# A mixer's input projections rewritten as one list of blocks: weight splits one block ahead, the gating half moved forward, the keys' products kept in PSUM

## The chip, the cores and the metric

The kernel runs on one core of a Trainium2 chip (trn2). The metric is device time in microseconds, from start to end of one execution; lower is better. Engines are named as the profile names them: PE is TensorE, DVE is VectorE, ACT is ScalarE, POOL is GpSimd, SP issues the DMAs. SBUF is the memory that the engines work in, PSUM the one that PE writes its products to; DVE and ACT can read and write both.

## The reference, cut to what matters

Two decoder layers over 512 tokens of width 1024. Layer 0 mixes tokens with `mixer_ab`; each layer then cross-attends into 256 memory tokens and applies a mixture of 32 experts.

```python
def mixer_ab(x, w_in, mu, w0, ..., w_out):
    p = x @ w_in                                  # 1024 -> 2816 columns
    ps = p[..., :AB_SHIFT_DIM]                    # r, k, v (512 each), w_lo, a_lo (64 each), g_lo (128)
    pu = p[..., AB_SHIFT_DIM:AB_SHIFT_DIM + SG_DIM]
    pv = p[..., AB_SHIFT_DIM + SG_DIM:]
    ps = ps + (token_shift(ps) - ps) * mu
    ya = rwkv7_mix(ps, ...)
    yb = spatial_gating(pu, pv, ln_g, ln_b, ws, bs)
    return jnp.concatenate([ya, yb], axis=-1) @ w_out

def spatial_gating(pu, pv, ln_g, ln_b, ws, bs):
    u = jax.nn.gelu(pu)
    z = jax.nn.gelu(pv).reshape(B, n_chunk, 128, 4, 128)
    z = layer_norm(z, ln_g, ln_b)                 # over each group of 128 channels
    zs = jnp.einsum('gts,bcsgd->bctgd', tril(ws), z) + bs.T[:, :, None]
    return u * zs.reshape(B, S, SG_DIM)

# in rwkv7_mix, per head of 64:
    kk = k * k_k; kk = kk / max(norm(kk), 1e-12)
    k = k * (1.0 + (a - 1.0) * k_a)
    state_t = state_{t-1} * decay - (state_{t-1} @ kk) (kk * a)^T + v k^T;   y_t = state_t @ r_t
```

## The kernel before

The program is written in Python against a tile layer, whose scheduler turns the order of the code and the dependencies into one queue for each engine. Each engine executes its queue strictly in order; an instruction at the head that waits for a semaphore holds all that stand behind it on that engine.

The change lies in the first 210 us: the first half of `mixer`. Precision comes from splitting: every fp32 operand becomes a high part (a cast on ACT, `wh`, `xh`) and a low part (a subtraction, `wl`, `xl`), and a product takes three matmuls, `xh*wh`, `xl*wh` and `xh*wl` (`mm3`, L212 to L214). A *block* here is one output of 128 columns by 512 tokens (or, in the token-major form, one slab of the contraction for four outputs): 24 matmuls of 512 columns. `wsplit` splits the weights of one block: ACT casts `wh` (L218), POOL subtracts `wl` (L219, since `k.lo_eng` is POOL in this stage). There are two buffers for split weights (`k.nsplit = 2`), so a split can run while the block before it is on PE.

Two generators share the stage and are stepped in turn. `filler` runs the projections: the block of `glo` (g_lo), four of r (`take_r`), four of v, and then `spatial`: the token-major projection `ptm` of the gating's second half (four slabs), GELU into `z`, mean and variance of its 16 groups (`bn_stats` L983, `bn_aggr` L984), an inverse root, the norm of z (L990 to L992), and four blocks of u with `gate`, whose matmuls `pz` (L999) take z. `late(...)` holds back what consumes a block's output until the next block's matmuls are written. `prep` builds the recurrence's operands and the inverse of a triangular matrix for each head and chunk:

- `pkk` (L839) spreads the inverse norms over the channels, four times, once for each group p of 128 channels; DVE multiplies (L841) into `kk`, an SBUF buffer of the ring `tmp` (five buffers), and from it makes `KR` (L842) and `Bn` (L846 with kk, L847 with `vv`); POOL makes `Kh` (L848);
- `pab` (L867) multiplies Bn and KR into `Aab`, 32 matrices of 128x128, copied by ACT (L869);
- the 32x32 diagonal blocks are inverted on DVE by a recurrence of 30 steps of two instructions (`pu` L892, `t8` L894), each waiting for the one before; it ends with a copy and two transposes (L898, L901, L900);
- `pC`, `pT`, `pC2`, `pN2`, `pT2` (L912 to L944) build the larger blocks of the inverse from these on PE, with copies by ACT and DVE between them.

`take_r` takes a block of r: ACT and DVE shift it (L758, L759) into `r`, DVE makes `bt` (L956), POOL scales KR (L957), and PE sums bt over the heads into `pbn` (L961). Those sums of the four blocks collect in one PSUM buffer, copied to `bon` after the last (L963).

PSUM has eight buffers in this stage: four with tag "a" (`prep`) and four with tag "b" (the projections, `pbn` and `pz`). Every `psum(...)` takes the next of its tag and waits until its last reader is done. The raw weights come through SP's queue, a megabyte at a time.

After the stage, `front(0)` begins the second half of the mixer with the transposes `ptv` (L1073). Everything behind that point is untouched: the mixer's second half, the cross-attention, and the experts, whose weights stream from memory while PE multiplies.

Of the kernel before, what the change touches and what calls it, by code (L numbers as in the profile page):

```python
# [714 lines left out]
def mixer(k):  # L715
# [6 lines left out]
    with ExitStack() as st:  # L722
# [18 lines left out]
        with ExitStack() as s1:  # L741
# [12 lines left out]
            def tmp(name):  # L754
                return pool.tile([P, T], F32, name=name, tag="tmp", bufs=5)
# [73 lines left out]
            def prep():  # L829
# [7 lines left out]
                for p in range(4):  # L837
                    ps = k.psum("a", name="pkk")
                    E.matmul(ps, selT[0:8, p * P:(p + 1) * P], rT[0:8, :], start=True, stop=True)  # L839
                    kk, kp = tmp("kk"), yb[:, p]  # L840
# [5 lines left out]
                    V.scalar_tensor_tensor(Bn[:, p], kk, -1.0, Bn[:, p], op0=ALU.mult, op1=ALU.mult)  # L846
                    V.tensor_tensor(Bn[:, p], Bn[:, p], vv[:, p], op=ALU.mult)  # L847
# [121 lines left out]
            def spatial():  # L969
                z = pool.tile([P, NT, 512], F32, name="z")  # L970
                wm = pool.tile([P, 4, P], F32, name="wm")
                nc.sync.dma_start(wm, A["sg_wsT"])
                zg = k.bcast(pool, A["sg_ln_g"], 512, "zg", tag="wa")
                zb = k.bcast(pool, A["sg_ln_b"], 512, "zb", tag="wa2")
                bs = k.bcast(pool, A["sg_b"], 512, "bs")
                yield from proj_tm(k, pool, w_in, 2304, xh, xl, NT, "b",
                                   lambda i, ps: S_.activation(z[:, i, :], ps, AF.Gelu_apprx_tanh))
                zst = pool.tile([P, 16, 6], F32, name="zst")
                zmv = pool.tile([P, 16, 2], F32, name="zmv")
                G_.tensor_tensor(wm, wm, tri[:, None, :].to_broadcast([P, 4, P]), op=ALU.mult)  # L980
                for i in range(NT):
                    for g in range(4):
                        V.bn_stats(zst[:, i * 4 + g], z[:, i, g * P:(g + 1) * P])  # L983
                        V.bn_aggr(zmv[:, i * 4 + g], zst[:, i * 4 + g])  # L984
                zr = k.rsqrt(pool, zmv[:, :, 1], 16, 1e-5, "zr")
                for i in range(NT):
                    for g in range(4):
                        n = i * 4 + g
                        s = z[:, i, g * P:(g + 1) * P]
                        V.tensor_scalar(s, s, zmv[:, n, 0:1], zr[:, n:n + 1], op0=ALU.subtract, op1=ALU.mult)  # L990
                    V.tensor_tensor(z[:, i], z[:, i], zg, op=ALU.mult)
                    V.tensor_tensor(z[:, i], z[:, i], zb, op=ALU.add)  # L992

                def gate(g, ps):
                    u = tmp("u")
                    S_.activation(u, ps, AF.Gelu_apprx_tanh)
                    pz = k.psum("b", name="pz")
                    for i in range(NT):
                        E.matmul(pz[:, i * P:(i + 1) * P], z[:, i, g * P:(g + 1) * P], wm[:, g, :], start=True, stop=True)  # L999
                    V.tensor_tensor(yb[:, g, :].rearrange("p (i t) -> p i t", i=NT), pz.rearrange("p (i t) -> p i t", i=NT),  # L1000
                                    bs[:, None, g * P:(g + 1) * P].to_broadcast([P, NT, P]), op=ALU.add)
                    G_.tensor_tensor(yb[:, g, :], yb[:, g, :], u, op=ALU.mult)

                yield from proj_cm(k, pool, w_in, 1792, 512, xh, xl, T, "b", late(gate))
                flush()

# [1177 lines left out]
```

## Time and profile before

| | |
|---|---|
| median of 3 runs | 1944.18 us (1942.24 to 1944.72) |
| the profiled execution's own time | 1946.41 us |
| its span, first to last instruction | 1944.6 us |
| PE busy | 1785.4 us, 92% of the span |
| DVE, ACT, POOL busy | 932.9, 527.8, 283.8 us |
| mean granted clock of PE | 0.965 of full speed |
| first half of the mixer | 0 to 209 us of the span |

A row of a timeline gives the start in us, the duration in us, the engine, the line of the kernel, the operation, what it writes and reads, and in brackets the idle time of that engine just before it and what ended that idle time. Matmuls are pipelined, so their durations overlap; the distance from start to start is what one costs.

### The profile page before, as it was taken

The numbers are of one execution on the slowest core, as the hardware profiler recorded it, in microseconds if no ns is written. First come the engines' busy times: TensorE is split into PE (matmuls) and PEld (weight loads), VectorE is DVE, ScalarE is ACT, GpSimd is POOL, SyncE is SP. The second block draws the span as 40 slices with busy tenths as digits, with TensorE's granted clock in tenths as the row PEclk, the third lists the DMA queues.
The fourth block names the chain that finished last, engine by engine and source line by source line (L and its number), as shares of the span: only waits on it lengthen the run. The fifth ranks groups of instructions, "written<-read, shape, count | busy, mean of one in ns | idle before, by whom it ended". The sixth has DMA issues, their size and how long they took to land. (4 is left out here: it accounts for less than half of the span.)

```text
span 1944.6 us, 23927 instructions
## 1 busy us (share of the span) xinstructions
PE 1785.4 (92%) x9222; PEld 1095.1 (56%) x9222; DVE 932.9 (48%) x2134; ACT 527.8 (27%) x989; POOL 283.8 (15%) x280
## 2 busy tenths in 40 slices
PE   8898989999889999989888999989979999998895
PEld 5687867878734443433338766768863434443432
DVE  5685366754723332332335666484572323332326
ACT  6333222343221111111122655343221111111110
POOL 3542532400100000000031100130020000000002
PEclk9898989999989999999999999999979999999997
DMA  5221017364889999999985200352779999999992
GB/s 190 65 66 55 23 48 233 115 202 164 346 335 418 420 420 420 419 420 419 418 317 174 76 12 23 109 174 87 290 290 386 421 419 419 419 420 420 421 417 99
DMA packets 126022, 514.69 MB, mean 265 GB/s; under 512 B 15520, under 2 KB 49472, under 8 KB 77264
## 3 DMA queue, kind: packets, MB, share of 16 engines
q1 hardware_dynamic: 115152, 486.60, 63.4%
q0 software_dynamic: 7056, 18.12, 2.8%
q10 hardware_dynamic: 3696, 8.41, 1.1%
q8 instruction: 74, 1.21, 0.3%
q14 instruction: 44, 0.36, 0.1%
HBM read 506.19 MB, written 14.70 MB: 268 GB/s over the span
## 5 line engine op out<-in xcount | busy, mean ns | idle before, releaser
L1787 PE MATMUL pu<-wu,xT 128*64 128x512 f32 x1024 | 237.8, 594 | 19.3 <-DMA wu<-in_moe_w_up_dram 19.3
L1787 PE MATMUL pg<-wg,xT 128*64 128x512 f32 x1024 | 231.6, 599 | 1.6 <-DMA wg<-in_moe_w_gate_dram 1.6
L1813 PE MATMUL py<-wd,hh 128*64 128x512 f32 x1024 | 229.3, 596 | 0.0
L1820 DVE SCALAR_TENSOR_TENSOR wy<-py,tab,wy 128x512 fp32r<-128x512 f32 x64 | 45.5, 747 | 284.1 <-ACT wy L1819 283.8
L1793 DVE TENSOR_TENSOR hh<-hh,pu 128x512 f32<-128x512 f32 x32 | 22.0, 688 | 317.0 <-PE pu L1787 317.0
L1787 PEld LDWEIGHTS pu<-wu,xT 128*64 128x64 f32 x1024 | 75.6, 137 | 174.4 <-issue 133.9
L1827 PE MATMUL pc<-wy,wc 128*128 128x512 f32 x480 | 139.9, 422 | 27.3 <-DVE h L1837 27.3
L1776 ACT ACTIVATE xT<-px,ch 128x128 f32<-128x128 f32 x128 | 48.2, 457 | 421.2 <-PE px L1769 383.5
L1787 PEld LDWEIGHTS pg<-wg,xT 128*64 128x64 f32 x1024 | 76.9, 138 | 149.0 <-issue 131.0
L1837 DVE TENSOR_TENSOR h<-h,pc 128x512 f32<-128x512 f32 x240 | 151.1, 681 | 8.6 <-PE pc L1827 8.6
L1813 PEld LDWEIGHTS py<-wd,hh 128*64 128x64 f32 x1024 | 71.2, 137 | 134.5 <-issue 129.7
L1827 PEld LDWEIGHTS pc<-wy,wc 128*128 128x128 f32 x480 | 81.6, 189 | 86.0 <-DVE h L1837 50.1
L1751 POOL DMA_INDIRECT xg<-rows,idx x32 | 33.5, 1046 | 528.9 <-PE px L1769 508.7
L1757 ACT ACTIVATE xg<-xg 128x1024 f32<-128x1024 f32 x32 | 39.7, 1240 | 246.5 <-DMA xg<-rows,idx 223.8
L218 ACT CAST wh<-wt 128x1024 fp32r<-128x1024 f32 x50 | 51.8, 1050 | 92.2 <-PE ptm L214 56.6
L219 DVE TENSOR_TENSOR wl<-wt,wh 128x1024 fp32r<-128x1024 f32 x37 | 48.1, 1306 | 58.3 <-ACT wh L218 57.9
L212 PE MATMUL ptm<-wh,oh 128*128 128x512 f32 x192 | 75.6, 394 | 0.0
L213 PE MATMUL ptm<-wl,oh 128*128 128x512 f32 x192 | 75.0, 391 | 0.0
L214 PE MATMUL ptm<-wh,ol 128*128 128x512 f32 x192 | 75.0, 390 | 0.0
L212 PE MATMUL pcm<-xh,wh 128*128 128x512 f32 x144 | 60.9, 423 | 7.9 <-ACT xh L218 6.9
L214 PE MATMUL pcm<-xh,wl 128*128 128x512 f32 x144 | 59.6, 414 | 0.5 <-DVE wl L219 0.5
L213 PE MATMUL pcm<-xl,wh 128*128 128x512 f32 x144 | 59.6, 414 | 0.2 <-DVE xl L219 0.2
(572 smaller groups left out, 3392.1 us busy)
## 6 DMA issues: line engine op xcount, KB each, us to landing
wg<-in_moe_w_gate_dram SPq DMA_DIRECT2D x128, 1024.0 KB
wu<-in_moe_w_up_dram SPq DMA_DIRECT2D x128, 1024.0 KB
wd<-in_moe_w_down_dram SPq DMA_DIRECT2D x124, 1024.0 KB
wr<-in_ab_w_in_dram SPq DMA_DIRECT2D x8, 1024.0 KB
wr<-in_xa_wkv_dram SPq DMA_DIRECT2D x8, 1024.0 KB
wt<-in_xa_wkv_dram SPq DMA_DIRECT2D x8, 1024.0 KB
wr<-in_xa_wq_dram SPq DMA_DIRECT2D x8, 1024.0 KB
wt<-in_xa_wo_dram SPq DMA_DIRECT2D x8, 1024.0 KB
```

The costliest lines, as they stand in the source:

```text
L212: nc.tensor.matmul(out, lh, rh, start=start, stop=False)
L213: nc.tensor.matmul(out, lh, rl, start=False, stop=False)
L214: nc.tensor.matmul(out, ll, rh, start=False, stop=stop)
L218: k.nc.scalar.copy(hi, src)
L219: (eng or k.low()).tensor_tensor(lo, src, hi.bitcast(F32), op=ALU.subtract)
L1757: self.k.nc.scalar.activation(x[:, :D], x[:, :D], AF.Identity, scale=x[:, D:D + 1], bias=x[:, D + 1:D + 2])
L1776: r = nc.scalar.activation(self.xT[:, kk, :], pk, AF.Identity, scale=gk, bias=bk)
L1787: nc.tensor.matmul(ps[j * M:(j + 1) * M, :], self.xT[:, half * 4 + kk, j * M:(j + 1) * M], w[j][:, kk, :], start=(half == 0 and kk == 0), ...
L1813: nc.tensor.matmul(py[n][j * M:(j + 1) * M, :], self.hT[:, half * 2 + kk, j * M:(j + 1) * M], w[j][:, kk, n * 512:(n + 1) * 512], start=(h ...
L1820: nc.vector.scalar_tensor_tensor(yl, py[n], self.tab()[:, 1:2], yh.bitcast(F32), op0=ALU.mult, op1=ALU.subtract)
L1827: self.k.nc.tensor.matmul(ps, self.C[:, i * P:(i + 1) * P], y, start=start and not last, stop=last)
L1837: k.nc.vector.tensor_add(k.h[:, i, s], k.h[:, i, s], pc)
```

## The change

Five things, all in the first half of `mixer`:

1. `kk` is a PSUM buffer of tag "a" instead of an SBUF buffer of `tmp`, and the products are taken in another order: `kk` is multiplied with `vv` in place, and then with Bn, so that each of the DVE instructions behind L841 has one operand in PSUM.
2. All remaining projections stand in one list of pairs (split, body): r, glo, the gating's second half (`ztm`), v, u. The block of glo moves behind r, and `ztm` moves from behind v to ahead of it.
3. Each block's split is written before the body of the block ahead of it.
4. Statistics and norm of z (`zstats`, `znorm`) are written behind the bodies of v's four blocks (list places 9 to 12), instead of behind the whole projection.
5. The mask of `wm` moves into the first body of `ztm`; statistics are written four at a time ahead of their `bn_aggr`.

```diff
-                    kk, kp = tmp("kk"), yb[:, p]
+                    kk, kp = k.psum("a", name="kk"), yb[:, p]
                     V.scalar_tensor_tensor(kk, Kh[:, p], col("k_k", p), ps, op0=ALU.mult, op1=ALU.mult)
                     V.tensor_tensor(KR[:, p, 0], kk, KR[:, p, 0], op=ALU.mult)
...
-                    V.scalar_tensor_tensor(Bn[:, p], kk, -1.0, Bn[:, p], op0=ALU.mult, op1=ALU.mult)
-                    V.tensor_tensor(Bn[:, p], Bn[:, p], vv[:, p], op=ALU.mult)
+                    V.scalar_tensor_tensor(kk, kk, -1.0, vv[:, p], op0=ALU.mult, op1=ALU.mult)
+                    V.tensor_tensor(Bn[:, p], kk, Bn[:, p], op=ALU.mult)
...
+            def cm(c0, ncols, consume):
+                raw = {}
+                def ops(cb):
+                    if cb % 2 == 0:
...
+                        raw[cb] = k.wchunk(w_in[:, s0:s0 + n].rearrange("(k p) n -> p k n", p=P), (KD, n), name="wr")
+                    return wsplit(k, pool, raw[cb - cb % 2][:, :, cb % 2 * P:cb % 2 * P + P], KD)
+                def body(cb, wh, wl):
+                    ps = k.psum("b", name="pcm")
+                    for kk in range(KD):
+                        mm3(nc, ps, wh[:, kk, :], wl[:, kk, :], xh[:, kk, :], xl[:, kk, :], kk == 0, kk == KD - 1)
+                    consume(cb, ps)
+                return [(partial(ops, cb), partial(body, cb)) for cb in range(ncols // P)]
...
+            def ztm():
...
+                def body(j, wh, wl):
+                    if j == 0:
+                        flush()
+                        sg["ps"] = [k.psum("b", name="ptm") for i in range(NT)]
+                        G_.tensor_tensor(sg["wm"], sg["wm"], tri[:, None, :].to_broadcast([P, 4, P]), op=ALU.mult)
...
+                    if j == 3:
+                        for i, ps in enumerate(sg["ps"]):
+                            S_.activation(sg["z"][:, i, :], ps, AF.Gelu_apprx_tanh)
...
+            def zstats(i):
+                for n in range(i * 4, i * 4 + 4):
+                    V.bn_stats(sg["zst"][:, n], sg["z"][:, i, n % 4 * P:n % 4 * P + P])
+                for n in range(i * 4, i * 4 + 4):
+                    V.bn_aggr(sg["zmv"][:, n], sg["zst"][:, n])
+                if i == 3:
+                    sg["zr"] = k.rsqrt(pool, sg["zmv"][:, :, 1], 16, 1e-5, "zr")
...
             def filler():
-                yield from proj_cm(k, pool, w_in, 1664, P, xh, xl, T, "b", late(take_g))
-                yield from proj_cm(k, pool, w_in, 0, 512, xh, xl, T, "b", late(take_r))
-                yield from proj_cm(k, pool, w_in, 1024, 512, xh, xl, T, "b", late(lambda p, ps: shifted(vv[:, p], ps, 8 + p)))
+                blocks = (cm(0, 512, late(take_r)) + cm(1664, P, late(take_g)) + ztm()
+                          + cm(1024, 512, late(lambda p, ps: shifted(vv[:, p], ps, 8 + p))) + cm(1792, 512, late(gate)))
+                after = {9: (zstats, 0, 1), 10: (zstats, 2, 3), 11: (znorm, 0, 1), 12: (znorm, 2, 3)}
+                w = blocks[0][0]()
+                for j, (_, body) in enumerate(blocks):
+                    ahead = blocks[j + 1][0]() if j + 1 < len(blocks) else None
+                    body(*w)
+                    w = ahead
+                    if j in after:
...
+                    yield
                 flush()
-                yield from spatial()
```

What the scheduler makes of it is shown at three places. Lines of the changed kernel are one higher than before down to the old `spatial` (L841 becomes L842).

PE, from the end of the third projection block after the keys to the next block (glo, r0, r1 are done before this place in the kernel before, r0, r1, r2 in the changed one). Before:

```order
L213 MATMUL pcm<-xl,wh 128x512
L214 MATMUL pcm<-xh,wl 128x512
L867 MATMUL pab<-Bn,KR 128x128 x10
L961 MATMUL pbn<-mixa,bt 128x2 x4
L867 MATMUL pab<-Bn,KR 128x128 x6
L212 MATMUL pcm<-xh,wh 128x512
```

The same place in the changed kernel:

```order
L214 MATMUL pcm<-xl,wh 128x512
L215 MATMUL pcm<-xh,wl 128x512
L868 MATMUL pab<-Bn,KR 128x128 x8
L962 MATMUL pbn<-mixa,bt 128x2 x4
L868 MATMUL pab<-Bn,KR 128x128 x8
L213 MATMUL pcm<-xh,wh 128x512
```

This `pbn` is that of r0 before and that of r1 now; r0's has moved up, behind the second of the three blocks, ahead of the third `pkk`.

DVE, the products of the third and fourth group of channels with the first r blocks. Before:

```order
L842 TENSOR_TENSOR KR<-kk,KR 128x512
L846 SCALAR_TENSOR_TENSOR Bn<-kk,Bn 128x512
L841 SCALAR_TENSOR_TENSOR kk<-Kh,cv,pkk 128x512
L847 TENSOR_TENSOR Bn<-Bn,vv 128x512
L842 TENSOR_TENSOR KR<-kk,KR 128x512
L846 SCALAR_TENSOR_TENSOR Bn<-kk,Bn 128x512
L759 SCALAR_TENSOR_TENSOR r<-pcm,cv,r 128x511
L847 TENSOR_TENSOR Bn<-Bn,vv 128x512
L956 SCALAR_TENSOR_TENSOR bt<-r,cv,yb 128x512
L759 SCALAR_TENSOR_TENSOR r<-pcm,cv,r 128x511
```

In the changed kernel:

```order
L843 TENSOR_TENSOR KR<-kk,KR 128x512
L847 SCALAR_TENSOR_TENSOR kk<-kk,vv 128x512
L842 SCALAR_TENSOR_TENSOR kk<-Kh,cv,pkk 128x512
L848 TENSOR_TENSOR Bn<-kk,Bn 128x512
L843 TENSOR_TENSOR KR<-kk,KR 128x512
L847 SCALAR_TENSOR_TENSOR kk<-kk,vv 128x512
L760 SCALAR_TENSOR_TENSOR r<-pcm,cv,r 128x511
L848 TENSOR_TENSOR Bn<-kk,Bn 128x512
L957 SCALAR_TENSOR_TENSOR bt<-r,cv,yb 128x512
L760 SCALAR_TENSOR_TENSOR r<-pcm,cv,r 128x511
```

The places are the same; in the three instructions behind each L842 `kk` now stands in PSUM.

DVE, the end of the recurrence and what follows it. Before, the recurrence runs out (only the shifts of r and v stand in it) and the statistics of z come behind all four copies of `pN`:

```order
L892 TENSOR_TENSOR pu<-pd_645,t_551 128x30
L894 TENSOR_TENSOR t_551<-t_551,pu 128x30
L898 COPY t_551<-t_551 128x32x32
L901 STREAM_TRANSPOSE b_550<-t_551 128x1024
L900 STREAM_TRANSPOSE b_550<-t_551 128x1024
L915 COPY t_551<-pC 32x512 x2
L925 COPY h<-pT 32x16x32 x2
L938 COPY t_551<-pN_1116 64x512
```

In the changed kernel:

```order
L1038 BN_STATS zst<-z 128x6
L893 TENSOR_TENSOR pu<-pd_656,t_562 128x30
L1038 BN_STATS zst<-z 128x6
L895 TENSOR_TENSOR t_562<-t_562,pu 128x30
L1038 BN_STATS zst<-z 128x6
L899 COPY t_562<-t_562 128x32x32
L902 STREAM_TRANSPOSE b_561<-t_562 128x1024
L901 STREAM_TRANSPOSE b_561<-t_562 128x1024
L760 SCALAR_TENSOR_TENSOR vv<-pcm,cv,vv 128x511
L1040 BN_AGGR zmv<-zst 128x2 x4
L1038 BN_STATS zst<-z 128x6 x4
L1040 BN_AGGR zmv<-zst 128x2 x4
```

Twelve of the sixteen BN_STATS and eight of the BN_AGGR now stand inside the recurrence's last eight steps, the first of them behind the L893 of 184 elements; the rest, the inverse root and the norm stand behind it, between the copies of `pC`, `pT` and `pN`.

## Rows read from the trace of the kernel before

**Rows 1.** Busy time by stretch: PE, PEld, DVE, ACT, POOL, PEclk, DMA share, GB/s

```profile
57.00:90.00 33.00, 25.94 (x112) 18.58 (x112) 25.87 (x36) 10.89 (x17) 19.93 (x13) 0.83 0.13 37
176.00:210.00 34.00, 29.13 (x138) 24.15 (x139) 20.11 (x41) 5.83 (x8) 9.62 (x5) 0.90 0.17 53
600.00:700.00 100.00, 96.00 (x450) 40.17 (x446) 34.63 (x70) 16.47 (x28) 3.78 (x7) 1.00 1.01 420
```

**Rows 2.** Timeline of PE, around the waits ahead of the block of r2

```profile
79.83 0.48 PE L867 MATMUL pab<-Bn,KR 64*128 64x128 f32 x2 [1.66 <-DVE kk L841]
85.62 1.87 PE L961 MATMUL pbn<-mixa,bt 128*128 128x2 f32 x8 [5.31 <-DVE bt L956]
...
89.01 0.79 PE L212 MATMUL pcm<-xh,wh 128*128 128x512 f32 x1
...
96.08 0.95 PE L961 MATMUL pbn<-mixa,bt 128*128 128x2 f32 x8
```

**Rows 3.** Timeline of DVE, the keys' products and the first r

```profile
66.62 0.75 DVE L841 SCALAR_TENSOR_TENSOR kk<-Kh,cv,pkk 128x512 f32<-128x512 f32 x1 [3.82 <-PE pkk L839]
...
83.23 0.68 DVE L847 TENSOR_TENSOR Bn<-Bn,vv 128x512 f32<-128x512 f32 x1
...
85.49 0.74 DVE L759 SCALAR_TENSOR_TENSOR r<-pcm,cv,r 128x511 f32<-128x511 f32 x1
86.27 2.06 DVE L956 SCALAR_TENSOR_TENSOR bt<-r,cv,yb 128x512 f32<-128x512 f32 x1
```

**Rows 4.** Timeline of POOL, one weight split in the same stretch

```profile
84.99 2.80 POOL L219 TENSOR_TENSOR wl<-wr,wh 128x1024 fp32r<-128x1024 f32 x1
```

**Rows 5.** Groups of DVE by form, 57 to 210 us: count, busy us, mean ns

```profile
L846 DVE SCALAR_TENSOR_TENSOR Bn<-kk,Bn 128x512 f32<-128x512 f32 x4 | 6.0, 1506 | 0.0
L842 DVE TENSOR_TENSOR KR<-kk,KR 128x512 f32<-128x512 f32 x4 | 6.0, 1495 | 0.0
...
L983 DVE BATCH_NORM_STATS2 zst<-z 128x6 f32<-128x128 f32 x16 | 4.2, 269 | 2.2 <-ACT z L977 2.2
...
L984 DVE BATCH_NORM_AGGREGATE zmv<-zst 128x2 f32<-128x6 f32 x16 | 2.5, 161 | 0.0
```

**Rows 6.** Timeline of ACT, the table load for glo's sigmoid

```profile
62.64 1.28 ACT L967 ACT_TABLE_LOAD   x1
```

**Rows 7.** Timeline of DVE, the recurrence: first step, r3, 184 elements, end

```profile
107.32 0.20 DVE L892 TENSOR_TENSOR pu<-pd,t 128x30 f32<-128x30 f32 x1
...
109.54 0.74 DVE L759 SCALAR_TENSOR_TENSOR r<-pcm,cv,r 128x511 f32<-128x511 f32 x1
...
128.58 0.36 DVE L892 TENSOR_TENSOR pu<-pd,t 128x184 f32<-128x184 f32 x1
...
136.80 1.19 DVE L900 STREAM_TRANSPOSE b<-t 128x1024 f32<-128x1024 f32 x1
```

**Rows 8.** Timeline of PE, the first pC and the first transpose behind the stage

```profile
138.16 3.63 PE L912 MATMUL pC<-b,Aab 32*32 32x32 f32 x122
...
209.12 0.60 PE L1073 MATMUL ptv<-cst,vv 128*128 128x128 f32 x4
```

**Rows 9.** Timeline of PE, the first pz and the block behind it

```profile
188.73 0.49 PE L999 MATMUL pz<-wm,z 128*128 128x128 f32 x2 [1.36 <-DVE z L992]
192.73 0.80 PE L999 MATMUL pz<-wm,z 128*128 128x128 f32 x2 [3.51 <-DVE z L992]
...
193.75 0.63 PE L213 MATMUL pcm<-xl,wh 128*128 128x512 f32 x1
194.18 0.63 PE L214 MATMUL pcm<-xh,wl 128*128 128x512 f32 x1
...
198.92 0.39 PE L212 MATMUL pcm<-xh,wh 128*128 128x512 f32 x1
199.15 0.40 PE L213 MATMUL pcm<-xl,wh 128*128 128x512 f32 x1
```

**Rows 10.** Groups of POOL by form, 57 to 210 us: the weight splits

```profile
L219 POOL TENSOR_TENSOR wl<-wr,wh 128x1024 fp32r<-128x1024 f32 x11 | 27.7, 2519 | 49.5 <-ACT wh L218 49.5
```

More of the change, by code (lines that the diff above doesn't have):

```diff
@@ L2 @@
 from contextlib import ExitStack, contextmanager
+from functools import partial
 from itertools import islice
@@ L967, in take_g @@
                 S_.activation(glo, glo, AF.Sigmoid)
[L969 to L1005, printed above, removed]
             pend = []
@@ L1018, in late @@
                 return take
-            def filler():
-                yield from proj_cm(k, pool, w_in, 1664, P, xh, xl, T, "b", late(take_g))
-                yield from proj_cm(k, pool, w_in, 0, 512, xh, xl, T, "b", late(take_r))
-                yield from proj_cm(k, pool, w_in, 1024, 512, xh, xl, T, "b", late(lambda p, ps: shifted(vv[:, p], ps, 8 + p)))
+            def cm(c0, ncols, consume):
+                raw = {}
+                def ops(cb):
+                    if cb % 2 == 0:
+                        n = min(2 * P, ncols - cb * P)
+                        s0 = c0 + cb * P
+                        raw[cb] = k.wchunk(w_in[:, s0:s0 + n].rearrange("(k p) n -> p k n", p=P), (KD, n), name="wr")
[6 more added lines that the diff above has]
+                return [(partial(ops, cb), partial(body, cb)) for cb in range(ncols // P)]
@@ new lines, in zstats, with znorm @@
+            def zstats(i):
[5 more added lines that the diff above has]
+                    sg["zr"] = k.rsqrt(pool, sg["zmv"][:, :, 1], 16, 1e-5, "zr")
+            def znorm(i):
+                z = sg["z"]
+                for n in range(i * 4, i * 4 + 4):
+                    t = z[:, i, n % 4 * P:n % 4 * P + P]
+                    V.tensor_scalar(t, t, sg["zmv"][:, n, 0:1], sg["zr"][:, n:n + 1], op0=ALU.subtract, op1=ALU.mult)
+                V.tensor_tensor(z[:, i], z[:, i], sg["zg"], op=ALU.mult)
+                V.tensor_tensor(z[:, i], z[:, i], sg["zb"], op=ALU.add)
@@ new lines, in gate @@
+            def gate(g, ps):
+                u = tmp("u")
+                S_.activation(u, ps, AF.Gelu_apprx_tanh)
+                pz = k.psum("b", name="pz")
+                for i in range(NT):
+                    E.matmul(pz[:, i * P:(i + 1) * P], sg["z"][:, i, g * P:(g + 1) * P], sg["wm"][:, g, :], start=True, stop=True)
+                V.tensor_tensor(yb[:, g, :].rearrange("p (i t) -> p i t", i=NT), pz.rearrange("p (i t) -> p i t", i=NT),
+                                sg["bs"][:, None, g * P:(g + 1) * P].to_broadcast([P, NT, P]), op=ALU.add)
+                G_.tensor_tensor(yb[:, g, :], yb[:, g, :], u, op=ALU.mult)
@@ new lines, in filler @@
+            def filler():
+                blocks = (cm(0, 512, late(take_r)) + cm(1664, P, late(take_g)) + ztm()
[7 more added lines that the diff above has]
+                    if j in after:
+                        f, *ii = after[j]
+                        for i in ii:
+                            f(i)
+                    yield
```

19 lines of the change are left out of this document (added).

## The prediction

> **What bounds the kernel now.** First I read the busy time by stretch [rows 1]: behind the mixer PE is busy 96 us of 100 and the weights stream at a DMA share of 1.01, so nothing there is touched or can be won. In the changed first half, two stretches stand out: 57 to 90 us, with PE busy 25.9 us of 33 at a mean granted clock of 0.83, and 176 to 210 us, 29.1 of 34 at 0.90; DMA is at 0.13 and 0.17, so no load binds. PE's queue is the line to follow: it is in order, and what ends last at its waits sets the time. Its timeline names those waits. At 79.83 PE has waited 1.66 us for a `kk` of DVE, and at 85.62 another 5.31 us for a `bt` of DVE [rows 2]; at 188.73 and 192.73 it has waited 1.36 and 3.51 us for the norm of z [rows 9]. After each pair the clock is at the lower level: matmuls of 512 columns start 0.43 us apart (193.75 to 194.18, 1.2 GHz), against 0.23 us (198.92 to 199.15, 2.4 GHz) [rows 9]. What PE did before the clock fell was to wait. Elsewhere in the stage PE runs through, and DVE's recurrence ends at 136.80 + 1.19 = 137.99 us [rows 7], just as PE reaches `pC` at 138.16 [rows 8]: before the change these two arrive together.
>
> **The products in PSUM.** Why is DVE late at 85.62? Its eight products L842 and L846 take 1.50 us on average [rows 5], while L847, as many elements, takes 0.68 when undisturbed [rows 3]. A split runs on POOL from 84.99 to 87.79 [rows 4]. Within it, L759, which reads PSUM, takes its usual 0.74 us, but L956, with two SBUF tensors, starts at 86.27 and ends at 88.33, after POOL is through [rows 3]. So a DVE instruction with two SBUF tensors stands still while POOL works, and one with a PSUM operand does not. The change gives all twelve products behind L841 a PSUM operand: 8 x (1.50 - 0.68) = 6.6 us go. The chain from the first L841 (66.62) to the fourth Bn (83.23 + 0.68 = 83.91) [rows 3] was 17.3 us; less 6.6, plus the shift and `bt` of r0 that now stand in it (0.7 and 0.7, up to 2.06 if POOL holds the second; I take 2.0 for both), it is 12.7. It starts some 1.5 us earlier, since glo's table load (1.28 us, [rows 6]) and sigmoid no longer stand on ACT ahead of the copy that `pkk` needs. Bn is complete near 77.8, r1's `bt` near 78.5.
>
> PE began to wait at 79.83 - 1.66 = 78.17. It now has one `pbn` more to do ahead of that (0.95 us, [rows 2]), so it comes by at 79 and finds both ready; I leave 0.3 us for a wait. Gone are 1.66 + 5.31 = 7.0 us, and the half clock behind them: 85.62 to 89.01 (`pbn` and six `pab`), half of 3.4 us, is 1.7, and the block from 89.01 to 96.08 took 7.07 us against 24 x 0.23 = 5.5, so 1.6 [rows 2]. Together 10.3 - 0.3 = **10.0 us**: what began at 96.08 begins at 86.1.
>
> An instruction with PSUM operands costs a little more: L841 0.75 against 0.68 for L847 [rows 3], 12 x 0.07 = 0.8 us, off PE's path, since DVE has 0.5 us in hand at each place and the loads of PE are three blocks. The Trainium skill speaks against working in PSUM ("VectorE: DVE Perf Modes", Rules for kernel authors: copy out of PSUM first if many operations follow). By that the products should go back to SBUF, and the 6.6 us would stay; the rows give 0.07 us for each as the price, so here the measurement decides.
>
> **Splits and loads moved ahead.** ACT's cast and POOL's subtraction (2.52 us, [rows 10]) of one block fit well into a block of 5.5 us; with two buffers, a split can't start before the block two places earlier is through, in either order. Cost nothing; if POOL falls a whole block behind, each block would wait up to 2.5 us. The loads keep their number and their places in SP's queue; the first raw tile of r grows to a full megabyte, with the DMA at 0.13 [rows 1]. The mask of `wm` moves on POOL behind a product that is read 30 us later: nothing.
>
> **The gating's second half moved up.** Its four outputs need all four "b" buffers. The third waits for the copy of `bon`, the fourth for the shift of glo, and both stand on DVE in the recurrence. The recurrence's first step follows the last `pab`, so it comes 10.0 us earlier, at 97.3 [rows 7]. glo's shift stands where r3's stood, 109.54 - 107.32 = 2.2 us in, and takes 0.74: 100.3. PE starts `ptm` near 95.5 (86.1, two `pbn`, 16 `pab` of 2 us in all, an estimate, and a block) and reaches the fourth output 18 x 0.23 later, at 99.6: a new wait of **0.7 us** (0 to 2.2).
>
> **Statistics inside the recurrence.** Here a wait is added that has no counterpart before: the first BN_STATS stands on DVE ahead of the last eight steps, and the recurrence's end, `pC` on PE, and everything behind it wait for that. When is z there? `ptm`'s first output is done after 72 + 6 matmuls, at 95.5 + 17.9 + 0.7 = 114.1; the table load (1.28, [rows 6]) and GELU make it 115.8. When does DVE get there? 128.58 - 107.32 = 21.3 us in [rows 7], less some 4.3 for four shifts and a `bt` that left (0.74 each, [rows 7], plus short waits), plus 0.7 for glo: 97.3 + 17.7 = 115.0. It waits 0.8 us. Then 137.99 - 128.58 = 9.4, less 1.0 for the last shift, plus the statistics: 12 x 0.27 + 8 x 0.16 = 4.5 us if each stands in the chain in full [rows 5], 0 if they fill the gaps between dependent steps; nothing in the rows decides, I take 2.3. The end is 115.8 + 8.4 + 2.3 = 126.5.
>
> PE arrives at `pC` at 138.16 - 10.0, less one `pbn` and eight matmuls that are now on the other side (0.9 + 1.8), plus 0.7: near 126.1. So it waits 0.4, and `pC` starts at **126.5**, 11.7 earlier.
>
> **From `pC` to the end of the stage.** That was 209.12 - 138.16 = 71.0 us [rows 8]. Add the eight matmuls, 1.8. In DVE's queue the norm of z now ends some 20 us (an estimate) ahead of `pz`, so 1.36 + 3.51 = 4.9 go, and with them the half clock of the block behind (eleven matmuls at 0.43 for 0.23, 2.2) [rows 9]: 65.7. `ptv` starts at **192.2**, 16.9 us earlier.
>
> **Behind the stage** no instruction changes place, and the first expert weights are issued by progress of the cross-attention, so all of it moves with `ptv`. The sum is made against the profiled execution, 1946.4 us: 1946.4 - 16.9 = 1929.5. That execution stands 2.2 us above the median of the runs, so the median of the changed kernel is **1927 us**. A measurement of this kernel tells about 0.2%, 4 us, from no change.
>
> **Rivals.** *The wait moves to DVE behind the recurrence* (0.18). The statistics cost their full 4.5 us (2.2 more), the third and fourth sets, the inverse root and the norm hold up the copies of `pC` and `pT` in DVE's queue, and PE's clock falls once more after such a wait (2.2, as behind `pz`, [rows 9]). For it: PE has nothing else to do while `pT` waits. Against: PE's own 3.6 us of `pC` [rows 8] cover most of it. 5 us less: 1932. The Trainium skill has a rule that makes it likelier ("SBUF — State Buffer", Who interferes with whom): a one-source DVE instruction in the two-port mode is blocked by POOL too, and POOL copies four pieces into `h` just then. No row here shows that pair; it is one more way to the same 1932.
>
> *PSUM doesn't free the products* (0.05): writing `kk` there costs, or the four "a" buffers make `pkk` and `pab` wait for `kk`. Then 9 of the 10.0 us stay: 1936. Against it: L759 beside the split [rows 3, 4].
>
> *Given back later* (0.05): the weights stream at full share [rows 1]; if their start were bound by something that doesn't move, PE would wait for them: 1944, no change.
>
> *Slower* (0.04): PE's clock stays at 1.2 GHz. Each of the new waits (0.3, 0.7, 0.4) is short, but if one of them drops the clock and it doesn't come back through `ptm` and v, each matmul costs 0.20 us more; 17 us are lost after 85 matmuls, three and a half blocks. Over seven blocks, 168 matmuls, 34 us: 1961. Against: the shortest waits behind which rows show the half clock are 1.36 and 3.51 together, and it came back within eleven matmuls.
>
> **How the numbers follow.** The forecast has 0.68, with its own range of 1924 to 1930 (statistics at 0 or 4.5, `ptm`'s wait at 0 or 2.2, a fall of the clock more or less). With the first rival to 1935, and 2 us on the other side for low-clock runs that vanish besides, the range is 1922 to 1935. Faster by over 0.2%: 0.68 + 0.18 + 0.05 = 0.91; within 0.2%: 0.05; slower: 0.04.
>
> **What would show it.** In the profile of the changed kernel: L843 and L847 (the products with `kk`) at 0.7 us on average; no wait of PE above 0.5 us at `pab` and `pbn`; r3's block at 0.23 us a matmul; a wait of the fourth `ptm` output for glo's shift below 1 us; `pC` at 126 to 128, waiting for DVE; no wait at `pz`; `ptv` near 192. The forecast is wrong if `pC` starts later than 130, if a granted clock below 0.9 shows between 86 and 126, or if `ptv` has moved 17 us and the end has not.

## The result, and the profile after

The changed kernel takes 1932.42 us in the median of four runs (1929.65 to 1937.78), beside 1944.45 us for the kernel before: a ratio of 0.9934 (95% interval 0.9915 to 0.9954), 12.0 us less. Two later series of the same kernel gave 0.9944 and 0.9950 (below); the median of the last, 1935.47, lies 0.5 above the forecast's range. The forecast was 1927, with 1922 to 1935 as its range and 1924 to 1930 as the likeliest case's own: the direction and the mechanism held, the narrower range was missed, and some 5 of the 17 us are missing.

The profiled execution of the changed kernel took 1937.78 us, the longest of its four (span 1935.8). First its waits. Timeline of PE in the changed kernel; columns: start, duration, engine, line, operation, output and inputs, wait:

```profile
81.91 1.16 PE L868 MATMUL pab<-Bn,KR 64*128 64x128 f32 x16
83.00 1.05 PE L962 MATMUL pbn<-mixa,bt 128*128 128x2 f32 x8
83.99 1.16 PE L868 MATMUL pab<-Bn,KR 64*128 64x128 f32 x16
...
90.67 0.95 PE L962 MATMUL pbn<-mixa,bt 128*128 128x2 f32 x8
...
104.95 0.50 PE L213 MATMUL ptm<-wh,xh 128*128 128x512 f32 x1 [0.64 <-DVE glo L760]
...
130.34 3.63 PE L913 MATMUL pC<-b,Aab 32*32 32x32 f32 x122
...
186.40 1.05 PE L1057 MATMUL pz<-wm,z 128*128 128x128 f32 x8
...
192.74 1.05 PE L1057 MATMUL pz<-wm,z 128*128 128x128 f32 x8
...
200.87 0.60 PE L1125 MATMUL ptv<-cst,vv 128*128 128x128 f32 x4
```

The waits of 1.66 and 5.31 us at `pab` and `pbn` [rows 2] and of 1.36 and 3.51 at `pz` [rows 9] are gone. The new wait at the fourth `ptm` output is 0.64 us (0.7 forecast), and `pC` starts without one (0.4 forecast). Yet `pbn` of r2 starts at 90.67, not 86.1, and `pC` at 130.34, not 126.5.

Now the products. Groups of DVE by form in the changed kernel, 57 to 210 us; behind the bar the busy us and the mean ns of one:

```profile
L1038 DVE BATCH_NORM_STATS2 zst<-z 128x6 f32<-128x128 f32 x16 | 4.3, 282 | 0.2 <-ACT z L1032 0.2
...
L847 DVE SCALAR_TENSOR_TENSOR kk<-kk,vv 128x512 f32<-128x512 f32 x4 | 2.7, 686 | 0.0
...
L848 DVE TENSOR_TENSOR Bn<-kk,Bn 128x512 f32<-128x512 f32 x4 | 2.7, 681 | 0.0
L843 DVE TENSOR_TENSOR KR<-kk,KR 128x512 f32<-128x512 f32 x4 | 2.7, 678 | 0.0
```

L843 and L847 take 0.68 and 0.69 us, where the products behind L841 took 1.50 [rows 5]. DVE waits 0.2 us for z in the recurrence, where the forecast had 0.8.

So no wait above 0.3 us is missing from the forecast (0.27 at `pT` is new). What differs is the clock. Timeline of PE in the changed kernel, among the fourth `pkk` and the block behind it:

```profile
72.44 2.02 PE L840 MATMUL pkk<-rT,mixa 8*128 8x512 f32 x2
...
75.41 0.63 PE L214 MATMUL pcm<-xl,wh 128*128 128x512 f32 x1
75.83 0.63 PE L215 MATMUL pcm<-xh,wl 128*128 128x512 f32 x1
```

These matmuls start 0.42 us apart (the lower level, 1.2 GHz) although PE had waited only 0.21 us since 54.57. Between `prn` and the first `pab`, 19 matmuls of 512 columns ran so, and this `pkk` took 2.02 us, where others take 1.12. In the kernel before there was none in this stretch. Between `pC` and the first `pz` there were 32, where the profile before showed 11. The 19 and the 21 more, 40 matmuls at 0.20 us each, make 8 us, and this execution is 8.7 behind the forecast (`ptv` at 200.87 for 192.2).

### The profile page after: what moved, and what is told of

It is laid out like the page before. It is cut to its first block, busy times and chain, and to the rows that moved or that the text cites. A ratio compares the mean times of both kernels' runs of the same rounds, so it can differ in the third digit from the quotient of the medians.

```text
span 1935.8 us, 23923 instructions
## 1 busy us (share of the span) xinstructions
PE 1785.1 (92%) x9222; PEld 1094.7 (57%) x9222; DVE 921.9 (48%) x2134; ACT 527.7 (27%) x989; POOL 280.0 (14%) x280
## 5 line engine op out<-in xcount | busy, mean ns | idle before, releaser
L1879 PEld LDWEIGHTS pc<-wy,wc 128*128 128x128 f32 x480 | 81.6, 189 | 86.1 <-DVE h L1889 50.2
```

The costliest lines, as they stand in the source:

```text
L1879: self.k.nc.tensor.matmul(ps, self.C[:, i * P:(i + 1) * P], y, start=start and not last, stop=last)
```

## The experiments

All times are medians; ratios are to the kernel before, run on the same chip in the same series. "Half-clock matmuls" are matmuls of 512 columns whose successor starts about 0.43 us later, counted in the one profile of each kernel.

| kernel | median us (runs) | before | ratio (95%) | half-clock: `prn`–`pab` | `pC`–`pz` | behind `pz` |
|---|---|---|---|---|---|---|
| before | 1944.45 (4) | | 1 | 0 | 11 | 11 |
| before again | 1944.33 (1) | 1946.79 | | 0 | 31 | 7 |
| changed | 1932.42 (4) | 1944.45 | 0.9934 (0.9915–0.9954) | 19 | 32 | 0 |
| changed, 2nd | 1932.79 (5) | 1945.54 | 0.9944 (0.9931–0.9958) | 0 | 28 | 0 |
| changed, 3rd | 1935.47 (8) | 1945.81 | 0.9950 (0.9935–0.9966) | 0 | 30 | 0 |
| products in SBUF | 1941.08 (12) | 1945.54 | 0.9978 (0.9968–0.9988) | 0 | 29 | 0 |
| only the products | 1939.96 (7) | 1945.54 | 0.9972 (0.9961–0.9983) | 0 | 23 | 6 |
| `kk` over `pkk` | 1935.07 (5) | 1945.54 | 0.9951 (0.9938–0.9964) | 6 | 27 | 0 |
| z behind v | 1934.82 (6) | 1946.79 | 0.9940 (0.9922–0.9958) | 0 | 12 | 11 |
| split not ahead | 1930.51 (6) | 1946.79 | 0.9926 (0.9904–0.9949) | 0 | 19 | 0 |
| spread | 1929.29 (6) | 1946.79 | 0.9920 (0.9899–0.9942) | 0 | 9 | 0 |
| spread, `pC` and `pT` too | 1926.56 (5) | 1945.81 | 0.9902 (0.9886–0.9917) | 21 | 6 | 0 |
| the same, `pn` behind r0 | 1935.80 (9) | 1945.81 | 0.9952 (0.9937–0.9968) | 10 | 8 | 0 |
| changed, `pn` behind r0 | 1942.90 (12) | 1945.81 | 0.9985 (0.9975–0.9995) | 10 | 31 | 0 |

No column covers the stretch from `pab` to `pC`. There five to nine ran at the half clock in both profiles of before, with the products in SBUF and in the last kernel but one, and at most one in the others.

**The same kernels again.** No edit.

> The changed kernel once more, unaltered. The theory (small matmuls): in the profiled execution of the changed kernel PE stood still for only 0.27 us (0.21 + 0.06) between 55 and 99 us, yet PE's granted clock fell twice between 65 and 80 us, each time behind keys' products `pkk` issued one at a time among a few large matmuls; if the order of the work sets this, this profile shows the half clock (0.43 us from matmul to matmul) in the same places, 65.8 to 69.2 and 72.4 to 79.3, and the time is 1930 to 1934. The rival (chance): the clock falls somewhere else in every execution; then the half-clock stretches stand in other places, and the median may be anywhere from 1928 to 1936.

> The changed kernel a third time, beside the kernels that move single steps in it. Theory (falls behind long runs of small matmuls are the rule, falls among the `pkk` are chance): its profile shows 20 to 32 half-clock matmuls between the first `pC` and `pT2`, 7 to 12 behind `pn`, and none or few at 65 to 80 us; its median is 1930 to 1933.5. Rival (the first profile of it was the typical one): 15 or more half-clock matmuls at 65 to 80 us, and 1934 to 1938.

> The kernel before once more, unaltered, for a second profile. In its first profile 13 matmuls of 512 columns ran at the half clock between the first `pC` and the end of `pT2`, and 11 behind `pz`; the kernel with only the products' change, which has the same order there, showed 24 and 6. Theory (where the clock falls is not the same in two executions): this profile shows another number, 18 to 30, between `pC` and `pT2`, and `ptv` moves with it, to 207 to 212 us. Rival (the order of work fixes it): 12 to 14 again, and `ptv` within 0.5 us of 209.1.

Windows of the kernel before, second profile: from the first `pn` to the first `pC`, to the first `ptv`, to the first router matmul (`plog`); columns: window, its length, busy us of PE, PEld, DVE, ACT, POOL with counts, mean granted clock, DMA share, GB/s:

```profile
53.99:135.77 81.78, 74.41 (x360) 58.82 (x360) 63.57 (x116) 29.33 (x38) 41.14 (x24) 0.92 0.20 65
135.77:210.42 74.65, 69.80 (x601) 58.68 (x600) 32.01 (x82) 20.08 (x26) 20.01 (x11) 0.82 0.12 37
210.42:511.70 301.28, 284.93 (x1811) 238.41 (x1810) 182.84 (x436) 97.69 (x170) 80.06 (x69) 0.98 0.47 161
```

The same three windows in the first profile of before:

```profile
55.91:138.16 82.25, 74.81 (x360) 59.09 (x360) 63.59 (x116) 29.32 (x38) 41.22 (x24) 0.92 0.20 64
138.16:209.12 70.96, 66.09 (x601) 55.86 (x601) 32.03 (x82) 20.09 (x26) 20.05 (x11) 0.88 0.12 39
209.12:511.70 302.58, 285.69 (x1811) 238.46 (x1810) 181.89 (x435) 97.74 (x170) 80.99 (x69) 0.97 0.46 161
```

In the changed kernel, first profile:

```profile
54.57:130.34 75.77, 74.92 (x352) 57.80 (x352) 56.58 (x133) 31.13 (x40) 36.84 (x23) 0.91 0.23 71
130.34:200.87 70.53, 70.26 (x608) 59.17 (x608) 28.86 (x66) 18.32 (x24) 19.95 (x12) 0.83 0.15 45
200.87:505.70 304.83, 287.27 (x1813) 239.47 (x1811) 181.87 (x436) 98.25 (x170) 80.91 (x69) 0.97 0.46 160
```

In the changed kernel, second series:

```profile
54.12:125.08 70.96, 70.13 (x352) 54.75 (x352) 56.45 (x133) 31.12 (x40) 36.92 (x23) 0.98 0.25 75
125.08:194.45 69.37, 68.80 (x609) 58.06 (x608) 28.86 (x66) 18.36 (x24) 19.97 (x12) 0.88 0.15 46
194.45:498.80 304.35, 287.16 (x1811) 239.38 (x1810) 181.78 (x436) 98.13 (x170) 80.93 (x69) 0.97 0.46 160
```

One kernel, unaltered, needed 75.77 us at a clock of 0.91 from `pn` to `pC` and 70.96 at 0.98; another needed 70.96 from `pC` to `ptv` at 0.88 and 74.65 at 0.82. The same instructions stand there in the same order, the waits agree within 0.3 us, and what differs by several microseconds is the granted clock. In the third series the two windows took 72.17 and 69.61 us; its half-clock counts are those that its theory expected, but its median, 1935.47, lies above the theory's range. So of the changed kernel's three executions one had the 19 half-clock matmuls among the `pkk` (the fully spread kernel below, with the same order there, shows 21), and the first profile of before was a favourable one behind `pC`. The theory that the place of the `pkk` fixes the fall of the clock fails here already: the second and third series issue them one by one and show no half clock. The Trainium skill ("TensorE: Matmul & The Clock Gate", What's actually happening) says that the number of matmuls at the lower clock at a kernel's start differs between runs of one kernel. These pairs of profiles show the like in the middle of one (19 and 0, 11 and 31).

**The products alone, and all but the products.** In the changed kernel:

```diff
-                    kk, kp = k.psum("a", name="kk"), yb[:, p]
+                    kk, kp = tmp("kk"), yb[:, p]
...
-                    V.scalar_tensor_tensor(kk, kk, -1.0, vv[:, p], op0=ALU.mult, op1=ALU.mult)
-                    V.tensor_tensor(Bn[:, p], kk, Bn[:, p], op=ALU.mult)
+                    V.scalar_tensor_tensor(Bn[:, p], kk, -1.0, Bn[:, p], op0=ALU.mult, op1=ALU.mult)
+                    V.tensor_tensor(Bn[:, p], Bn[:, p], vv[:, p], op=ALU.mult)
```

> The changed kernel with `kk` in SBUF again and the three products as they were before. Of the prediction's first step this is the price: the products behind L842 go back from 0.68 to about 1.5 us when POOL works, so the fourth Bn is complete some 6.6 us later, near 85, and PE, which reaches `pab` at 81.9 in the changed kernel, waits again 3 to 4 us at `pab` and `pbn` and loses some 2 us more to the half clock behind. In this kernel the `pkk` come in pairs, as they did before the change. Theory (pkk one at a time cost the clock): the 4.9 us of half clock between 65 and 80 go, so the net is 0 to +2 us against the changed kernel, 1932 to 1934.5. Rival (the half clock there has nothing to do with pkk's places): +5 to +6 us, 1937 to 1939.

and the reverse of this edit in the kernel before:

> The kernel before with only the products' change: `kk` in PSUM and the three products reordered. By the prediction's first step the waits of 1.66 and 5.31 us at `pab` and `pbn` go, with 3.3 us of half clock behind them, 10 us in all: 1934.5; the waits of 1.36 and 3.51 at `pz` stay. Theory (pkk one at a time cost the clock): here too they no longer come in pairs, so some 3 to 5 us of half clock appear between 63 and 78 us and the gain is 5 to 7: 1937.5 to 1939.5. Rival (no such cost): 1934 to 1935.

Taking PSUM out costs 8.3 us against the changed kernel on the same chip (1941.08 to 1932.79); putting it into the kernel before gains 5.6 (1945.54 to 1939.96). 1941.08 is above both expected ranges; 1939.96 is 0.5 us above the theory's, without the half clock among the `pkk` that the theory needed. With only the products `pC` comes 72.74 us behind `pn`, where before took 82.25, so the forecast's 10 us are nearly all there; part of it is lost again, behind `ptv` (303.7 us to `plog`, for 302.6 and 301.3) and, against the first profile of before, from `pC` to `ptv` (73.89 for 70.96). What holds DVE is seen in the first of the two. POOL there:

```profile
68.52 2.79 POOL L220 TENSOR_TENSOR wl<-wr,wh 128x1024 fp32r<-128x1024 f32 x1
```

and DVE in the same execution, a product of two SBUF tensors:

```profile
69.03 2.83 DVE L847 SCALAR_TENSOR_TENSOR Bn<-kk,Bn 128x512 f32<-128x512 f32 x1
```

It ends at 71.86, 0.55 us after POOL's split, as L956 did in [rows 3, 4]; in the changed kernel none of these products took more than 0.76. PE then waits 4.81 us at `pbn`, with seven half-clock matmuls behind it. The Trainium skill ("SBUF — State Buffer", Who interferes with whom) states that a DVE instruction with two SBUF inputs contends with a POOL instruction that reads SBUF, and that the contention is an exclusive lock. These rows agree: 2.83 us instead of 0.68, ended 0.55 us behind the split.

**`kk` written over `pkk`.**

```diff
-                    kk, kp = k.psum("a", name="kk"), yb[:, p]
+                    kk, kp = ps, yb[:, p]
```

> The changed kernel with `kk` written over `pkk` in the same PSUM buffer, so that two `pkk` need no other buffer to come free and PE issues them in pairs again; on PE nothing else changes place. Theory (pkk one at a time cost the clock): the half clock at 65.8 to 69.2 and 72.4 to 79.3 goes or shrinks to one run, 3 to 4.9 us less than the changed kernel: 1927.5 to 1929.5. Rival (the fall is set by something else, or by chance): within 1 us of the changed kernel, and half-clock runs still in that stretch.

The `pkk` came in pairs, six half-clock matmuls showed between them and `pab`, and the median was 1935.07 beside 1932.79, with overlapping intervals. Pairs are no remedy, and the theory's 3 to 4.9 us less did not come; the rival's "within 1 us" was missed by 1.3.

**z behind the values again.**

```diff
-                blocks = (cm(0, 512, late(take_r)) + cm(1664, P, late(take_g)) + ztm()
-                          + cm(1024, 512, ...) + cm(1792, 512, late(gate)))
-                after = {9: (zstats, 0, 1), 10: (zstats, 2, 3), 11: (znorm, 0, 1), 12: (znorm, 2, 3)}
+                blocks = (cm(0, 512, late(take_r)) + cm(1664, P, late(take_g))
+                          + cm(1024, 512, ...) + ztm() + cm(1792, 512, late(gate)))
+                after = {12: (zstats, 0, 1, 2, 3), 13: (znorm, 0, 1, 2, 3)}
```

> The changed kernel with the gating's second half behind the values again, its statistics and norm all behind it, the list and the products kept. This takes back the prediction's third step. Theory: PE waits again 1.36 and 3.51 us at `pz` for the norm of z and loses 2 us of half clock behind, 7 us; the waits at the fourth `ptm` (0.62) and at `pT` (0.3 to 0.6) go: 5.5 to 6.5 us more than the changed kernel, 1938 to 1939. Rival (the clock gives it back, since PE rests less and falls elsewhere less): 1934 to 1936.

PE at the first group of `pz`, with the wait back in one piece:

```profile
181.57 0.80 PE L1057 MATMUL pz<-wm,z 128*128 128x128 f32 x2 [4.22 <-DVE z L1050]
```

and the windows from `pC` to `ptv` and on to `plog`:

```profile
126.43:197.98 71.55, 67.29 (x602) 56.54 (x602) 31.98 (x82) 20.00 (x26) 20.71 (x12) 0.88 0.12 39
197.98:500.60 302.62, 285.50 (x1811) 238.74 (x1810) 181.66 (x435) 97.74 (x170) 80.89 (x69) 0.97 0.47 161
```

The wait of 4.22 us and eleven half-clock matmuls are back, but the time isn't: the ratio, 0.9940, lies between those of the three series of the changed kernel. From `pC` to `ptv` this order loses only 1.0 to 2.2 us, since 12 matmuls instead of 28 to 32 ran at the half clock ahead of `pz`; behind `ptv` it needs about 2 us less. That the move of z brings 7 us by itself isn't borne out; its worth is not resolved from zero. This is the rival's number.

**The split at the block itself.**

```diff
-                w = blocks[0][0]()
-                for j, (_, body) in enumerate(blocks):
-                    ahead = blocks[j + 1][0]() if j + 1 < len(blocks) else None
-                    body(*w)
-                    w = ahead
+                for j, (ops, body) in enumerate(blocks):
+                    body(*ops())
```

> The changed kernel with each block's loads and split issued at the block itself, not one block ahead; on PE nothing changes place. The prediction put this part at nothing, since with two buffers for the split one stands ready anyway. Theory: within 1.5 us of the changed kernel, 1931 to 1934, and no wait of PE for a `wl` above 0.3 us. Rival (splits come late behind POOL's and ACT's other work): waits of up to 2.5 us at two to five blocks, 1936 to 1944.

1930.51 us, and no wait for a `wl` behind 54 us: the split ahead brings nothing that can be measured, as forecast (no series of the changed kernel stands beside it, and its interval overlaps all three). This profile also shows what half clock costs when a wait follows. Here the block behind `pn` ran at the full clock, and PE then waited for DVE:

```profile
60.63 0.60 PE L834 MATMUL prn<-cst,rny 128*8 128x128 f32 x4 [1.79 <-DVE rny L147]
```

With seven half-clock matmuls in that place, the second series of the changed kernel started `prn` at 60.52. There the half clock cost nothing, since DVE's norm set the start.

**The small matmuls spread.** The changed kernel with `yield` behind each `pC2`/`pN2` pair and each `pT2` instead of each second one, and blocks cut in halves:

```diff
                         mm3(nc, ps, wh[:, kk, :], wl[:, kk, :], xh[:, kk, :], xl[:, kk, :], kk == 0, kk == KD - 1)
+                        if kk == KD // 2 - 1:
+                            yield
...
-                    body(*w)
+                    for _ in body(*w):
+                        if j > 10:
+                            yield
...
-                    if n % 2:
-                        yield
+                    yield
```

> The changed kernel with the small matmuls of the inverse spread: PE does 16 of `pC2`/`pN2` and then 12 matmuls of a block, four times, and 16 of `pT2` and then 12, four times; before it was 32 and then 24, and 32 and then 24. The work is the same. Theory (a long run of small matmuls brings the clock down for the large ones behind it): of the 27 to 32 matmuls at half clock between 134 and 168 us fewer than 12 are left, 3 to 5 us less than the changed kernel: 1927.5 to 1929.5. Rival (the share of small matmuls counts, not their grouping, or chance): 20 or more half-clock matmuls stay, 1931 to 1934.

> The spread kernel with the small matmuls of `pC` and `pT` spread too: 9 matmuls of a block, half of `pC`, 3, the other half, 12, half of `pT`, 12, the other half, 12, and on as there. In every profile so far 6 to 12 matmuls behind `pT` ran at the half clock (in the spread kernel 10), and PE waited 0.3 to 0.6 us for DVE at `pT`. Theory (a long run of small matmuls brings the clock down): no half-clock run is left between the first `pC` and `ptv`, 2 us less than the spread kernel: 1927 to 1928. Rival (the fall behind `pT` has another cause): 8 or more half-clock matmuls stay, 1929 to 1931.

The second of the two also yields behind each half of `pC` and of `pT`, cuts the blocks from `j > 9` on, and takes a few steps of the two generators by hand ahead of `interleave` (the same 352 matmuls stand between `pn` and `pC`):

```diff
+            for n in (1, 1):
+                next(fl)
+                next(pr)
+            next(fl)
             interleave(fl, pr)
```

PE behind 48 small matmuls in the changed kernel's second series:

```profile
143.46 0.67 PE L937 MATMUL pN<-cst,h 64*64 64x64 f32 x8
...
145.01 0.63 PE L213 MATMUL pcm<-xh,wh 128*128 128x512 f32 x1
145.43 0.63 PE L214 MATMUL pcm<-xl,wh 128*128 128x512 f32 x1
```

and behind 24 in the first spread kernel:

```profile
148.28 0.67 PE L937 MATMUL pN<-cst,h 64*64 64x64 f32 x8
148.88 0.50 PE L213 MATMUL pcm<-xh,wh 128*128 128x512 f32 x1
149.22 0.40 PE L214 MATMUL pcm<-xl,wh 128*128 128x512 f32 x1
149.46 0.40 PE L215 MATMUL pcm<-xh,wl 128*128 128x512 f32 x1
```

In the eleven profiles that keep the long runs, the clock fell behind every `pT` and behind 19 of the 22 runs of `pC2` and `pN2`, with at most 0.6 us of waiting ahead of a fall. At `pT` PE waited 0.3 to 0.6 us in seven of the eleven, and not at all in the other four (both of before, only the products, z behind v), where the clock fell too; the second expectation's "0.3 to 0.6 us" in every profile does not hold for those. In the three with spread work it fell behind no group of `pC2`, `pN2` or `pT2` and behind no half of `pT`; what remains is one fall, behind the uncut `pT`, or behind the second half of `pC`, which follows the first after only three large matmuls (six at the half clock there). So the theory's "no half-clock run is left" failed by that one. And not every long run is followed by a fall. PE in the first profile of before, 64 `pT2` (L944) in one run:

```profile
171.88 3.94 PE L944 MATMUL pT<-b,t 64*64 64x64 f32 x64
175.75 0.50 PE L212 MATMUL pcm<-xh,wh 128*128 128x512 f32 x1
176.09 0.39 PE L213 MATMUL pcm<-xl,wh 128*128 128x512 f32 x1
176.32 0.40 PE L214 MATMUL pcm<-xh,wl 128*128 128x512 f32 x1
```

None came behind these 64 in any of the three profiles that have them, nor behind the 32 `pT2` in the other eight. So the number of small matmuls in a run doesn't decide by itself; what does is open.

From `pC` to `ptv` the fully spread kernel needs 65.49 us at a clock of 0.97:

```profile
129.95:195.44 65.49, 65.49 (x609) 54.25 (x608) 33.05 (x66) 18.25 (x24) 20.02 (x12) 0.97 0.17 48
```

The prediction's 65.7 for this stretch was thus the price of the work at the full clock. With 1926.56 us the fully spread kernel is 8.9 us ahead of the changed one on the same chip, and the intervals don't touch: it beats both kernels. The last two rows of the table repeat the difference, 1935.80 beside 1942.90. In the profiles of the fully spread and the third changed kernel only part of the 8.9 us can be placed, 4.1 from `pC` to `ptv` (65.49 for 69.61) and 1.3 from there to `plog` (303.1 for 304.4), since the profiled execution of the spread one, 1933.88 us, was its slowest. The first spread kernel had no series of the changed kernel beside it, and its interval overlaps theirs.

**The norm sums behind the whole block of r0.** In both kernels the matmuls of the fourth `pn` are kept back (`last_n`) and issued behind the first block of the list:

```diff
+            next(fl)
+            last_n[0]()
             next(pr)
-            for n in (2, 2, 2, 2):
-                next(fl)
+            for q, n in enumerate((2, 2, 2, 2)):
+                if q:
+                    next(fl)
```

> The changed kernel with only the fourth `pn` behind the whole block of r0. Theory (waiting brings the clock down): no wait of 2.3 us at `pn` and no half clock behind it, in the profile too; against the changed kernel 1 to 2.5 us less (1930 to 1931.5), the rest taken back by a wait of about 2 us for `bt` at `pbn`. Rival (the fall behind `pn` is the small `pn` matmuls' doing or chance): the half-clock run of 7 to 12 matmuls stays behind `pn`, and the time is 1931.5 to 1933.

> The kernel with everything spread, and with the fourth head pair's norm sums (`pn`, the wait of 2.3 us for `sq`) behind the whole block of r0 instead of behind 14 of its 24 matmuls. Theory: the wait goes, since the ten matmuls fill it, and with it the 7 to 12 half-clock matmuls behind it (1.4 to 2.4 us); PE comes to the keys' products up to 3.9 us earlier, but DVE, whose chain starts from the same `pn`, has the second `bt` ready only 23.3 us after `pn`, so PE waits there about 2 us: net 1 to 2.5 us less than the kernel without this, 1925 to 1927. Rival (DVE's chain takes all of it back): within 0.5 us of it.

Both expectations failed: 7.4 and 9.2 us more than without the edit. The wait at `pn` went, and with it the half-clock run behind it, but a larger wait came one step on. PE in the first of them:

```profile
62.96 1.02 PE L842 MATMUL prn<-cst,rny 128*8 128x128 f32 x4 [5.08 <-DVE rny L147]
```

DVE at the end of the norm:

```profile
60.46 0.19 DVE L145 SCALAR_TENSOR_TENSOR rnt<-rnt,rnx 128x32 f32<-128x32 f32 x1
60.69 2.22 DVE L147 SCALAR_TENSOR_TENSOR rny<-rnt,rny 128x32 f32<-128x32 f32 x1
```

and POOL under it:

```profile
60.50 2.35 POOL L220 TENSOR_TENSOR wl<-wr,wh 128x1024 fp32r<-128x1024 f32 x1 [1.77 <-ACT wh L219]
```

The last step of the inverse root, 32 columns of two SBUF tensors, takes 2.22 us instead of 0.19, because it has come to lie under a split. Behind the wait ten large matmuls and two `pkk` (2.0 us each) run at the half clock. That the clock is down behind a long wait is seen here; that filling the wait at `pn` would help was wrong, since DVE's chain from `pn` to `prn` (54.12 to 60.52, 6.4 us, in the changed kernel's second series) was the bound, and the hold made it longer.

## Why the prediction was right, and where it was off

**The products** held: 1.50 to 0.68 us each, no wait at `pab` and `pbn`; the chain to the fourth Bn took 12.97 us (63.13 to 76.10) in the second series for 12.7, and PSUM alone brings `pC` from 82.25 us behind `pn` to 72.74. With the rest of the change it is 70.96 in the second series; the forecast's 126.5 − 55.91 is 70.6. The 0.07 us that an operand in PSUM was to cost measured at most 0.02.

**Splits ahead** cost and bring nothing that can be measured, as said. **`ptm`'s wait** was 0.62 to 0.64 us for 0.7. **The statistics** cost 0.9 us for the 2.3 taken: they fill the gaps of the dependent chain, so a step takes 0.44 us with one between, beside 0.39 without. From the step of 184 elements to the copy behind the last one it was 119.96 to 126.15, less 0.25 of waiting, 5.9 us; before, 128.58 [rows 7] to 134.67, less 1.0 for a shift, 5.1. That copy itself took 1.82 us for 1.15: the rows below show it begin under a split and end 0.99 us behind it, where before it began 0.92 us ahead of the split. It reads one SBUF tensor, and the first rival said of such an instruction beside POOL that no row shows it; here one does (its mode no run shows). It cost nothing, since `pC` starts without a wait. DVE in the changed kernel:

```profile
121.22 0.33 DVE L893 TENSOR_TENSOR pu<-pd,t 128x168 f32<-128x168 f32 x1
121.45 0.29 DVE L1038 BATCH_NORM_STATS2 zst<-z 128x6 f32<-128x128 f32 x1
121.66 0.32 DVE L895 TENSOR_TENSOR t<-t,pu 128x168 f32<-128x168 f32 x1
...
126.15 1.82 DVE L899 COPY t<-t 128x1024 f32<-128x1024 f32 x1
```

and POOL under the copy:

```profile
124.58 2.40 POOL L220 TENSOR_TENSOR wl<-wr,wh 128x1024 fp32r<-128x1024 f32 x1 [3.48 <-ACT wh L219]
```

**From `pC` to the end of the stage** is the step that was mis-sized. The 71.0 us of [rows 8] were taken as work plus the waits at `pz`; they held eleven half-clock matmuls ahead of `pz`, and the second profile of before held 31 and took 74.65. By the prediction's own working that profile gives 74.65 + 1.8 − 4.9 − 1.4 = 70.2, and the three profiles of the changed kernel show 70.5, 69.4 and 69.6, for 65.7 forecast. The rival "the wait moves to DVE behind the recurrence" gave the right time, 1932, but by luck in the main: its statistics were to cost their full 4.5 us and cost 0.9; the clock falls once more, but no long wait stands ahead of it (0.3 to 0.6 us at `pT`), and before the change it fell there as well. "Slower" (the clock stays down through `ptm` and v) did not come: the granted clock is 1.00 from 81 to 125 us in the first profile.

**From `pn` to `pC`** the first profile lost another 4.8 us to the clock and the third 1.2; on average 73.0 us for the 70.6 forecast. By the prediction's own sign, `pC` later than 130, the first profile spoke against it (130.34); in the second and third series it came at 125.08 and 126.28.

**Behind the stage** not everything moved with `ptv`: from there to `plog` the two profiles of before took 302.6 and 301.3 us, the three of the changed kernel 304.8, 304.4 and 304.4. PE is busy for 285.7 and 284.9 us of it before, 287.3 and 287.2 in the first two after, with the same instructions in the same order, and its idle time there grows by 0.3 to 1.2 us. So most of this too looks like the clock: 1.4 to 1.8 us of it stand in the `pmq` matmuls, the first eight of which start 0.185 us apart for 0.100 before. With z behind v it was 302.6, and with only the products 303.7, so some 2 us of the gain come and go with what stands ahead. Why is open.

Averaged over these profiles (two of before, three of the changed kernel), the account is −0.7 ahead of `pn`, −9.0 to `pC`, −3.0 to `ptv` and +1.6 behind: −11.1 us, beside 12.0, 12.8 and 10.3 less in the medians of the three series. How the gain divides between the list and the products isn't fully settled either: the products alone give 5.6, the list without them 4.5, and z's place nothing that can be measured, though the waits at `pz` are real.

## What to carry to other kernels

A sum over one profiled execution takes that execution's clock for part of the work: before a saving of a few microseconds is forecast, count the matmuls at the half clock in the stretch, and ask for a second profile. Where an engine waits for DVE while POOL is busy, look whether DVE's instruction has two SBUF tensors; an operand in PSUM frees it. Where the large matmuls behind a long run of small ones show the lower clock though PE never waits, cut the run up among the large ones and measure: here that took most of the falls away.

## What the runs showed of the hardware

A busy PE is no guard of its clock: behind 122 `pC` and 126 `pT` (32 by 32) or 48 of `pC2` and `pN2` (64 by 64), with 0.6 us of waiting at most, 5 to 13 large matmuls ran at 1.2 GHz in nearly every profile; behind groups of 16 or 24 small ones between stretches of 12 large ones none did, nor behind 64 `pT2` (64 by 64) in one run. (Counts of small ones are the profile's.) The same program fell at 65 to 80 us in one execution (19 matmuls) and not in two others. A DVE instruction of 32 columns took 2.22 us instead of 0.19 under a POOL split of 2.35, and one of 512 columns 2.83 for 0.68 under one of 2.79: in both the hold lasted for the rest of POOL's instruction. A DVE copy from one SBUF tensor, begun 1.57 us into a split, took 1.82 us for 1.15.
